# Order of the seven block products of a channel pair in the SwiGLU up-projection: t1 third, and in the first pair h22 ahead of t3

## Chip, cores and metric

One core of one Trainium2 chip. The metric is the device time of one execution in microseconds (us); the kernel before was run three times.

## The reference, cut to what matters

One decoder layer: a Mamba-2 and a sparse-attention mixer, an output projection, a layer norm, and a SwiGLU channel mixer with a causal convolution of width 3, for 1024 tokens, width 1024 and 2816 gate and 2816 up channels, in float32.

```python
def _conv_ffn(h, w_up, conv_w, conv_b, w_down):
    u = _causal_dwconv(h @ w_up, conv_w, conv_b)
    gate, up = jnp.split(u, 2, axis=-1)
    return (jax.nn.silu(gate) * up) @ w_down
```

The change lies in how `h @ w_up` is computed.

## The kernel before, in words

**The product.** `h @ w_up` is done by a scheme of the Strassen-Winograd kind with seven block products in place of eight. The blocks of h are h11 and h21 (tokens 0 to 511, the two halves of the 1024 inputs), h22 (the second half of the inputs for tokens 512 to 1023) and the differences t1 (block 4 to 7 less block 0 to 3, first half of the inputs), t2, t3 and t4. The blocks of the weights are, for each of 22 channel pairs j (128 gate columns g and 128 up columns u), the halves of g and u and the sums of them that `w_prep` forms on VectorE: s13 = (u0 + u1, g0 - u0), s24 = (s13's first - g0, g1 - s24's first), in lines 1051 to 1054.

**Precision.** Every operand is split into a high part (a rounded copy, on ScalarE) and a low part (the difference, on VectorE or GpSimd). A product is four input blocks of 128, each with three matmuls of 128x128 by 128x512 (`three`, lines 159 to 161), so 12 matmuls, and 84 a pair. `w_split` (lines 956 to 962) splits one weight block: ScalarE line 960, GpSimd line 961.

**Banks.** A pair uses a bank `pa` for h11 and h21 (`first`), `pb` for t2, `pc` for t3 and t4, and `pd` for t1 and h22. The first product in `pc` or `pd` is read by VectorE, and then the second is accumulated onto it in the same bank. These readings (evictions) are issued by `now` (line 978), with a priority 300 places ahead of their place in the program. Their results u2 and u3 lie in 128x512 buffers of the tag "s2", of which there are five; c1 (line 984), hr, d1, d3 and d4 use the same tag.

**Before the pairs.** The second part of the layer norm makes h for eight token blocks (lines 991 to 1043) and writes the operands h11, h21, t1, t2, h22 with `put`: line 922 on ScalarE, line 923 on VectorE or GpSimd. `first` of pairs 0 and 1 is already issued there, and `w_prep(0)` follows. Lines 1066 to 1072 then make t3 (d3, line 1069, VectorE) and t4 (d4, line 1071, GpSimd) from t2's raw values and h_raw.

**Weights and buffers.** `up_load` (line 938) loads the raw g and u of a pair, 512 KB each, on SP's queue, into three buffers of the tag "wr". `w_split` number n takes its buffer by a list (the lines quoted first below), three buffers of "wh", three of "wl" and eight of "pp", of which t1 holds four, and h_raw four until the d4 that reads it is done. Numbers 0 to 3 are the halves of g of pairs 0 and 1, so pair 0's other five blocks are numbers 4 to 8 in the order of the loop in `w_prep`, with the tags wh, wl, wh, wl, pp.

```python
WTAG = ("tx", "tx", "wh", "wl", "wh", "wl", "wh", "wl", "pp", "pp", "wh", "wl", "pp", "pp")
t = big("w_hl", F32R, (P, 2, 512), WTAG[n] if n < 4 else WTAG[4 + (n - 4) % 10])
```

**Order.** A planner fixes each engine's instruction order ahead of the run: it walks through its own timeline of the program and gives a free engine the instruction of highest priority (earliest in the program) that is ready in that timeline. SP's queue alone keeps the order of the program. On the chip each engine works through its queue in the fixed order.

**After the products** of a pair, `conv_half` (lines 1074 to 1084) takes a bias and three taps (ScalarE line 1078, VectorE line 1082 twice) of `xu` and `xg`, for each half of 512 tokens, then SiLU (line 1115) and the product with the up half (line 1116). Every second pair also forms sums of the gated values on VectorE and GpSimd (lines 1125 to 1136) and stores them for the down-projection.

Of the kernel before, what the change touches and what calls it, by code (L numbers as in the profile page):

```python
# [13 lines left out]
OP = mybir.AluOpType  # L14
# [43 lines left out]
def hybrid_layer(ctx, tc, x, w_in, ssd_conv_w, ssd_conv_b, dt_bias, a_log, d_skip, ssd_norm_g,  # L58
                 idx_k_norm_g, idx_k_norm_b, w_out, ln1_g, ln1_b, w_up, ffn_conv_w, ffn_conv_b,
                 w_down, ln2_g, ln2_b, out):  # L60
    nc = tc.nc
# [15 lines left out]
    def big(name, dtype=F32, shape=(P, 1024), tag="t4"):  # L77
        return pool.tile(list(shape), dtype, name=name, tag=tag, bufs=BUFS[tag])

    def bank(name, tag, shape=(P, 512)):  # L80
        return psum.tile(list(shape), F32, name=name, tag=tag, bufs=PBUFS[tag])
# [4 lines left out]
    def mid(name, dtype=F32, shape=(P, 512), tag="s2"):  # L86
        return pool.tile(list(shape), dtype, name=name, tag=tag, bufs=S2 if tag == "s2" else EV)

    def f(t):
        return t.bitcast(F32)  # L90
# [67 lines left out]
    def three(ps, ah, al, bh, bl, start, stop, onto=False):  # L158
        nc.tensor.matmul(ps, ah, bh, start=start, stop=False, skip_group_check=onto)  # L159
        nc.tensor.matmul(ps, ah, bl, start=False, stop=False, skip_group_check=onto)  # L160
        nc.tensor.matmul(ps, al, bh, start=False, stop=stop, skip_group_check=onto)  # L161
# [269 lines left out]
    def next_w(ahead=1):  # L431
        load_ahead(1)
        w = ready.pop(0)
        load_ahead(ahead)
        return w
# [3 lines left out]
    for t in range(4):  # L439
        w = w_qi if t == 0 else next_w()  # L440
        a, c = big("qsa", F32R, tag="pp"), big("qsb", F32R, tag="pp")
# [472 lines left out]
    def operand(name, tag):  # L914

        return [[big(name + p, F32R, (P, 2, 512), tag) for _ in range(2)] for p in "hl"]
# [17 lines left out]
    def pair_of(n):  # L934

        return n // 2 + n % 2 * (NF // 2)

    def up_load(j, parts=(0, 1)):
        if j < NF:
            raws.setdefault(j, [])  # L940
            ct = pair_of(j)
            for s in parts:
                raw = big("w_raw", tag="wr", shape=(P, NK, P))
                nc.sync.dma_start(raw, bass.AP(tensor=w_up.tensor, offset=w_up.offset + s * DFF + ct * P,
                                               ap=[[2 * DFF, P], [P * 2 * DFF, NK], [1, P]]))
                raws[j].append(raw)

    def up_gate(j):

        g = raws[j][0].rearrange("p (k2 k) n -> p k2 (k n)", k2=2)  # L950
        return [w_split(g[:, k2]) for k2 in range(2)]
# [4 lines left out]
    def w_split(src):  # L956
        n = count["w"]
        count["w"] += 1
        t = big("w_hl", F32R, (P, 2, 512), WTAG[n] if n < 4 else WTAG[4 + (n - 4) % 10])
        nc.scalar.activation(t[:, 0], src, AF.Copy)  # L960
        nc.gpsimd.tensor_tensor(t[:, 1], src, f(t[:, 0]), op=OP.subtract)  # L961
        return t
# [8 lines left out]
    def product(ps, w, h, start):  # L971

        for k in range(4):
            ks = slice(k * P, (k + 1) * P)
            three(ps, w[:, 0, ks], w[:, 1, ks], h[0][k // 2][:, k % 2], h[1][k // 2][:, k % 2],
                  start and k == 0, k == 3, not start)

    def now(call, *a, **k):
        with tc.high_priority(EV_PRIO):
            call(*a, **k)  # L980

    def first(j, w):

        a, c1 = bank("pa", "ip"), mid("c1")
        product(a, w[0], h11, True)
        now(nc.scalar.activation, c1, a, AF.Copy)
        product(a, w[1], h21, False)
        return a, c1

    firsts = {}  # L990
    for i, b in enumerate(LN_ORDER):
# [7 lines left out]
        if i == 4:  # L999
            t2_raw += [big("t2raw", tag="tx") for _ in range(2)]  # L1000
            h22, t1, t2 = operand("h22", "t4"), operand("t1", "pp"), operand("t2", "t4")
            up_load(0)
        if i == 5:
            gates = {0: up_gate(0)}
# [42 lines left out]
    def w_prep(j):  # L1047

        g, u = (t.rearrange("p (k2 k) n -> p k2 (k n)", k2=2) for t in raws.pop(j))
        s13, s24 = big("s13", tag="pt", shape=(P, 2, 512)), big("s24", tag="pt", shape=(P, 2, 512))  # L1050
        nc.vector.tensor_tensor(s13[:, 0], u[:, 0], u[:, 1], op=OP.add)
        nc.vector.tensor_tensor(s24[:, 0], s13[:, 0], g[:, 0], op=OP.subtract)
        nc.vector.tensor_tensor(s13[:, 1], g[:, 0], u[:, 0], op=OP.subtract)
        nc.vector.tensor_tensor(s24[:, 1], g[:, 1], s24[:, 0], op=OP.subtract)
        if j not in gates:
            gates[j] = [None, None]
        out = []
        for src, w in ((g[:, 0], gates[j][0]), (s24[:, 0], None), (g[:, 1], gates[j][1]), (s13[:, 1], None),
                       (s13[:, 0], None), (u[:, 1], None), (s24[:, 1], None)):
            out.append(w or w_split(src))  # L1060
        return out

    ws = {0: w_prep(0)}
    up_load(1, (1,))
    t3, t4 = operand("t3", "wo"), operand("t4", "wo")
# [8 lines left out]
    def conv_half(x_, tag, ct, half):  # L1074

        v_ = bank("v", tag)
        o = half * 512
        nc.scalar.activation(v_, x_[:, o:o + 512], AF.Identity, bias=fw[:, 132 + ct:133 + ct], scale=fw[:, 88 + ct:89 + ct])
        for sft in (1, 2):
            tap = fw[:, (2 - sft) * 44 + ct:(2 - sft) * 44 + ct + 1]  # L1080
            z = 0 if half else sft
            nc.vector.scalar_tensor_tensor(v_[:, z:], x_[:, o - sft + z:o + 512 - sft], tap, v_[:, z:],
                                           op0=OP.mult, op1=OP.add)
        return v_

    for j in range(NF):
        if j:
            up_load(j + 1)
        w = ws.pop(j)
        a, c1 = firsts.pop(j) if j in firsts else first(j, (w[0], w[2]))  # L1090
        bb = bank("pb", "pv")
        product(bb, w[1], t2, True)
        xg, xu, gt = big("xg", tag="tx"), big("xu", tag="tx"), big("gt", tag="t4")
        u2 = mid("u2")
        now(nc.vector.tensor_tensor, u2, c1, bb, op=OP.add)
        now(nc.scalar.activation, xg[:, :512], a, AF.Copy)
        c = bank("pc", "tp")
        product(c, w[3], t3, True)
        u3 = mid("u3")
        now(nc.vector.tensor_tensor, u3, u2, c, op=OP.add)  # L1100
        d = bank("pd", "lg")
        product(d, w[4], t1, True)
        now(nc.vector.tensor_tensor, xu[:, 512:], u3, d, op=OP.add)
        product(c, w[5], t4, False)
        now(nc.vector.tensor_tensor, xu[:, :512], u2, c, op=OP.add)
        product(d, w[6], h22, False)
        now(nc.vector.tensor_tensor, xg[:, 512:], u2, d, op=OP.add)
        if j + 1 < NF:
            ws[j + 1] = w_prep(j + 1)
        cg, cu = pair_of(j), NF + pair_of(j)  # L1110
        for half in range(2):
            hs = slice(half * 512, half * 512 + 512)
            vu = conv_half(xu, "lg", cu, half)
            vg = conv_half(xg, ("ip", "tp")[half], cg, half)
            nc.scalar.activation(gt[:, hs], vg, AF.Silu)
            nc.vector.tensor_tensor(gt[:, hs], gt[:, hs], vu, op=OP.mult)
        rows = slice(j // 2 * P, (j // 2 + 1) * P)
        if j % 2 == 0:
            v1 = gt
            nc.scalar.dma_start(g_dr[rows, 0], v1[:, :512])  # L1120
        else:
            lo1, hi1, lo2, hi2 = v1[:, :512], v1[:, 512:], gt[:, :512], gt[:, 512:]
            nc.scalar.dma_start(g_dr[rows, 1], lo2)
            q1, q2 = mid("q1", tag="ev"), mid("q2", tag="ev")
            nc.vector.tensor_tensor(q1, hi1, hi2, op=OP.add)
            nc.vector.tensor_tensor(q2, q1, lo1, op=OP.subtract)
            q3, q4 = hi1, lo1
            nc.gpsimd.tensor_tensor(q3, lo1, hi1, op=OP.subtract)
            nc.gpsimd.tensor_tensor(q4, lo2, q2, op=OP.subtract)
            nc.scalar.dma_start(g_dr[rows, 2], q4)  # L1130
            for n, (q, hi) in enumerate(((q1, xu[:, :512]), (q2, xu[:, 512:]), (q3, xg[:, :512]), (hi2, xg[:, 512:]))):
                hi, lo = hi.bitcast(F32R), q.bitcast(F32R)
                nc.scalar.activation(hi, q, AF.Copy)
                nc.gpsimd.tensor_tensor(lo, q, f(hi), op=OP.subtract)
                nc.scalar.dma_start(gs_dr[rows, 0, n], f(hi))
                nc.scalar.dma_start(gs_dr[rows, 1, n], f(lo))
# [107 lines left out]
    c1, u2 = ([x[t // 2][:, t % 2] for t in range(4)] for x in (cu, uu))  # L1244
    u3 = c1
# [79 lines left out]
```

## Time and profile before

| what | value |
|---|---|
| three runs, us | 1696.53, 1702.73, 1699.14; median 1699.14 |
| the profiled execution, us | 1697.82 |
| its span, first to last instruction, us | 1695.9 |
| mean granted TensorE clock over the span | 0.974 of 2.4 GHz |
| TensorE matmul busy | 1595.1 us, 94% |
| VectorE busy | 1250.8 us, 74% |
| ScalarE busy | 926.1 us, 55% |
| GpSimd busy | 896.0 us, 53% |

The products of the 22 pairs run from about 1009 us to 1466 us of the span; the down-projection follows to the end. In the rows, times are from the start of the span. Engines: PE is TensorE, PEld its weight load, DVE VectorE, ACT ScalarE, POOL GpSimd, SPq SP's DMA queue. "out<-in" names the tiles; a bracket at the end of a row gives the engine's idle time before it and what ended that. Names are shortened in the records: `s` is s13 or s24, `d` is d1, d3 or d4 (the line tells which), `u` is u2 or u3.

### The profile page before, as it was taken

What the parts mean: (1) busy time and instruction counts of PE and PEld (TensorE: products, weight loads), DVE (VectorE), ACT (ScalarE), POOL (GpSimd) and SP (SyncE); (2) the same over time, 40 slices, a digit from 0 to 9 for tenths busy, and PEclk for the clock granted to TensorE, in tenths of its full rate; (3) what the DMA queues carried; (4) which work ended last, traced back from release to release, by engine and by line L of the source; (5) the groups of instructions that cost most, each with busy time, mean ns of one, the idle gap of its engine ahead of it and who ended that gap; (6) DMA issues with size and microseconds to landing.
All of it is one profiled execution on the core that took longest, in us unless ns stands there. A gap on an engine that the chain in (4) does not pass through costs nothing.

```text
span 1695.9 us, 23283 instructions
## 1 busy us (share of the span) xinstructions
PE 1595.1 (94%) x7844; PEld 1318.0 (78%) x7844; DVE 1250.8 (74%) x2262; ACT 926.1 (55%) x1809; POOL 896.0 (53%) x669
## 2 busy tenths in 40 slices
PE   8999998897989989999999995999999999989997
PEld 6888887685878867777888774888888788868886
DVE  2644689999894457787787579668777777678668
ACT  3433597687732576676676465555455555542141
POOL 2153225534168253555464448586776667576590
PEclk9999999997999999999999997999999999999999
DMA  5042032132423563554454461243433333698782
GB/s 173 10 129 63 13 106 85 41 99 57 140 83 108 176 200 108 148 156 133 137 156 156 140 193 55 94 137 130 147 122 118 118 128 117 220 371 304 234 283 106
DMA packets 208590, 232.86 MB, mean 137 GB/s; under 512 B 14035, under 2 KB 138327, under 8 KB 208471
## 3 DMA queue, kind: packets, MB, share of 16 engines
q1 hardware_dynamic: 161031, 159.80, 31.3%
q10 hardware_dynamic: 47440, 71.58, 11.5%
q8 instruction: 62, 1.02, 0.3%
q14 instruction: 57, 0.47, 0.1%
HBM read 159.71 MB, written 71.63 MB: 136 GB/s over the span
## 4 chain that ended last, share of the span: by engine, by line
PE 67%; DVE 20%; DMA 4%; ACT 4%; issue 3%; POOL 2%; ACTq 0%; SPq 0%; DVEq 0%; POOLq 0%
PE proj L159 4%; PE proj L161 4%; PE proj L160 4%; PE acc L160 4%; PE acc L161 4%; PE acc L159 4%; DVE junk L347 3%; PE ops L159 3%; PE ops L160 3%; PE ops L161 3%; PE ptp L692 3%; PE pc L160 2%; PE pc L161 2%; PE pc L159 2%; PE pd L159 2%
## 5 line engine op out<-in xcount | busy, mean ns | idle before, releaser
L159 PE MATMUL proj<-xTh,w_hi 128*128 128x512 f32 (+1 forms) x432 | 173.1, 401 | 7.2 <-ACT xbc L478 4.6
L161 PE MATMUL proj<-xTh,w_lo 128*128 128x512 f32 (+1 forms) x432 | 170.5, 396 | 3.0 <-POOL w_lo L132 3.0
L686 POOL TENSOR_SCALAR prob<-prob,sm 128x512 f32<-128x512 f32 (+7 forms) x128 | 96.5, 763 | 143.9 <-DVE sm L685 109.2
L160 PE MATMUL proj<-xTl,w_hi 128*128 128x512 f32 (+1 forms) x432 | 171.2, 397 | 0.0
L961 POOL TENSOR_TENSOR w_hl<-s,w_hl 128x512 fp32r<-128x512 f32 x88 | 119.4, 1364 | 72.1 <-ACT w_hl L960 68.9
L129 POOL TENSOR_SCALAR w_hi<-w_raw 128x1024 fp32r<-128x1024 f32 x35 | 44.3, 1267 | 184.3 <-PE proj L160 125.5
L132 POOL TENSOR_TENSOR w_lo<-w_raw,w_hi 128x1024 fp32r<-128x1024 f32 (+1 forms) x45 | 112.5, 2503 | 27.7 <-ACT w_hi L131 25.5
L160 PE MATMUL acc<-wd_hl,g_hl 128*128 128x512 f32 x308 | 121.6, 395 | 3.6 <-POOL wd_hl L1205 3.6
L161 PE MATMUL acc<-wd_hl,g_hl 128*128 128x512 f32 x308 | 121.2, 394 | 0.0
L683 ACT ACTIVATE prob<-prob,mx 128x512 f32<-128x512 f32 (+7 forms) x128 | 98.4, 770 | 36.5 <-DVE mx L680 35.8
L694 ACT ACTIVATE pt<-ptp 128x512 fp32r<-128x512 f32 x144 | 81.2, 594 | 64.8 <-PE ptp L692 43.5
L159 PE MATMUL acc<-wd_hl,g_hl 128*128 128x512 f32 x308 | 112.6, 393 | 2.8 <-ACT wd_hl L1204 2.7
L961 POOL TENSOR_TENSOR w_hl<-w_raw,w_hl 128x512 fp32r<-128x512 f32 x66 | 91.2, 1386 | 41.7 <-ACT w_hl L960 40.8
L1205 POOL TENSOR_TENSOR wd_hl<-keep,wd_hl 128x512 fp32r<-128x512 f32 x55 | 92.0, 1704 | 33.9 <-ACT wd_hl L1204 33.9
L159 PE MATMUL ops<-w_hi,y_hi 128*128 128x512 f32 x256 | 104.2, 407 | 5.6 <-ACT y_hi L131 3.1
L350 ACT ACTIVATE junk<-score,cand 128x1024 bf16<-128x1024 f32 (+2 forms) x96 | 86.0, 896 | 39.7 <-DVE cand L364 36.7
L695 DVE TENSOR_TENSOR pt<-ptp,pt 128x512 fp32r<-128x512 f32 x144 | 95.5, 684 | 15.1 <-ACT pt L694 14.8
L159 PE MATMUL tps<-w_hi,xTh 128*128 128x256 f32 x320 | 96.0, 301 | 9.8 <-ACT tout L614 8.7
L160 PE MATMUL ops<-w_lo,y_hi 128*128 128x512 f32 x256 | 102.8, 402 | 0.4 <-DVE w_lo L132 0.4
L159 PEld LDWEIGHTS proj<-xTh,w_hi 128*128 128x128 f32 (+1 forms) x432 | 82.0, 190 | 27.0 <-ACT xbc L478 5.4
L161 PE MATMUL ops<-w_hi,y_lo 128*128 128x512 f32 x256 | 100.4, 396 | 0.0
L161 PEld LDWEIGHTS proj<-xTh,w_lo 128*128 128x128 f32 (+1 forms) x432 | 81.6, 189 | 21.2 <-POOL w_lo L132 4.2
(344 smaller groups left out, 5057.8 us busy)
## 6 DMA issues: line engine op xcount, KB each, us to landing
w_raw<-in_ffn_w_up_dram SPq DMA_DIRECT2D x44, 512.0 KB, 3.9
g_hl<-gs_dr SPq DMA_DIRECT2D x44, 512.0 KB, 5.0
w_raw<-in_w_in_dram SPq DMA_DIRECT2D x36, 512.0 KB, 4.4
r_dr<-rout ACTq DMA_DIRECT2D x48, 256.0 KB, 2.3
g_dr<-gt ACTq DMA_DIRECT2D x33, 256.0 KB, 2.9
keep<-in_ffn_w_down_dram SPq DMA_DIRECT2D x33, 256.0 KB, 6.1
acsb<-a_dr SPq DMA_DIRECT2D x16, 512.0 KB, 4.1
w_raw<-in_w_out_dram SPq DMA_DIRECT2D x16, 512.0 KB, 3.8
```

The costliest lines, as they stand in the source:

```text
L132: (nc.vector if lo_on_dve else nc.gpsimd).tensor_tensor(lo, raw, f(hi), op=OP.subtract)
L159: nc.tensor.matmul(ps, ah, bh, start=start, stop=False, skip_group_check=onto)
L160: nc.tensor.matmul(ps, ah, bl, start=False, stop=False, skip_group_check=onto)
L161: nc.tensor.matmul(ps, al, bh, start=False, stop=stop, skip_group_check=onto)
L347: nc.vector.tensor_scalar(junk[0][:, :n], top[b] if k >= 16 and b in top else score_ap[b], c, None, op0=OP.is_lt, op1=OP.add, accum_out=va ...
L350: nc.scalar.activation(junk[1][:, :n], score_ap[b], AF.Sign, bias=c, scale=-1.0, accum_out=val[e][:, i:i + 1])
L683: nc.scalar.activation(t[:, :w], t[:, :w], AF.Exp, bias=mx[:, h:h + 1], scale=-1.0, accum_out=sm[:, h:h + 1])
L686: nc.gpsimd.tensor_scalar(t[:, :w], t[:, :w], sm[:, 4 + h:5 + h], 1.0, op0=OP.mult, op1=OP.mult)
L694: nc.scalar.activation(pt[:, 0], ps, AF.Copy)
L695: nc.vector.tensor_tensor(pt[:, 1], ps, f(pt[:, 0]), op=OP.subtract)
L961: nc.gpsimd.tensor_tensor(t[:, 1], src, f(t[:, 0]), op=OP.subtract)
L1205: nc.gpsimd.tensor_tensor(wt[:, 1], w_raw, f(wt[:, 0]), op=OP.subtract)
```

## The change

The loop in `w_prep` splits the weight blocks in another order, and the pair loop issues the products in another order. Before: t2, t3, t1, t4, h22 (behind h11 and h21). After: t2, t1, t3, h22, t4; in pair 0: t2, t1, h22, t3, t4. u3 is now u2 plus the t1 product, where it was u2 plus the t3 product. The last product of a pair is t4, whose eviction writes `xu[:, :512]`; before it was h22, whose eviction writes `xg[:, 512:]`. The instructions are as many as before.

```diff
-        for src, w in ((g[:, 0], gates[j][0]), (s24[:, 0], None), (g[:, 1], gates[j][1]), (s13[:, 1], None),
-                       (s13[:, 0], None), (u[:, 1], None), (s24[:, 1], None)):
+        for src, w in ((g[:, 0], gates[j][0]), (s24[:, 0], None), (g[:, 1], gates[j][1]), (s13[:, 0], None),
+                       (s24[:, 1], None), (s13[:, 1], None), (u[:, 1], None)):
             out.append(w or w_split(src))
         return out
...
         now(nc.scalar.activation, xg[:, :512], a, AF.Copy)
+        d = bank("pd", "lg")
+        product(d, w[3], t1, True)
+        u3 = mid("u3")
+        now(nc.vector.tensor_tensor, u3, u2, d, op=OP.add)
         c = bank("pc", "tp")
-        product(c, w[3], t3, True)
-        u3 = mid("u3")
-        now(nc.vector.tensor_tensor, u3, u2, c, op=OP.add)
-        d = bank("pd", "lg")
-        product(d, w[4], t1, True)
-        now(nc.vector.tensor_tensor, xu[:, 512:], u3, d, op=OP.add)
-        product(c, w[5], t4, False)
+        if j:
+            product(c, w[5], t3, True)
+            now(nc.vector.tensor_tensor, xu[:, 512:], u3, c, op=OP.add)
+        product(d, w[4], h22, False)
+        now(nc.vector.tensor_tensor, xg[:, 512:], u2, d, op=OP.add)
+        if not j:
+            product(c, w[5], t3, True)
+            now(nc.vector.tensor_tensor, xu[:, 512:], u3, c, op=OP.add)
+        product(c, w[6], t4, False)
         now(nc.vector.tensor_tensor, xu[:, :512], u2, c, op=OP.add)
-        product(d, w[6], h22, False)
-        now(nc.vector.tensor_tensor, xg[:, 512:], u2, d, op=OP.add)
```

## Rows read from the trace of the kernel before

**Rows 1.** Windows: length, busy us (x instructions) by engine, clock, DMA share, GB/s

```profile
1041.00:1062.14 21.14, 10.91 (x27) 7.06 (x26) 18.57 (x18) 8.04 (x22) 20.08 (x16) 0.68 0.09 26
...
1062.14:1338.00 275.86, 275.84 (x1215) 227.47 (x1213) 207.65 (x285) 150.39 (x247) 191.70 (x144) 1.00 0.38 128
```

**Rows 2.** Waits of PE, 1030 to 1470 us: total us, times, longest

```profile
PE pc L159 <- ACT t3h L922: 6.5, 1, 6.5
...
PE pb L160 <- DVE t2l L923: 2.9, 1, 2.9
PE pd L159 <- DVE xg L980: 1.6, 1, 1.6
PE pb L161 <- POOL w_hl L961: 1.1, 1, 1.1
```

**Rows 3.** Timeline of PE: start us, us, engine, line, operation

```profile
1057.07 0.79 PE L159 MATMUL pc<-t3h,w_hl 128*128 128x512 f32 x1 [6.51 <-ACT t3h L922]
...
1062.14 0.39 PE L159 MATMUL pb<-t2h,w_hl 128*128 128x512 f32 x1
...
1064.86 0.39 PE L159 MATMUL pd<-h22h,w_hl 128*128 128x512 f32 x1
...
1070.52 0.39 PE L159 MATMUL pb<-t2h,w_hl 128*128 128x512 f32 x1
```

**Rows 4.** Chain of waits: start us, its share of the chain in us, what

```profile
1039.80 0.75 DVE s L1051
...
1041.15 0.60 DVE s L1053
...
1048.66 1.14 DVE s L1052
...
1051.49 1.13 DVE s L1054
1052.62 2.28 DVE t3l L923 x2
...
1056.60 0.42 ACT t3h L922
```

**Rows 5.** Timeline of POOL

```profile
1017.08 1.71 POOL L961 TENSOR_TENSOR w_hl<-w_raw,w_hl 128x512 fp32r<-128x512 f32 x1
...
1042.85 0.90 POOL L923 TENSOR_TENSOR h22l<-hr,h22h 128x256 fp32r<-128x256 f32 x1
1043.71 1.44 POOL L961 TENSOR_TENSOR w_hl<-s,w_hl 128x512 fp32r<-128x512 f32 x1
```

**Rows 6.** Timeline of DVE

```profile
1047.92 0.75 DVE L923 TENSOR_TENSOR t3l<-d,t3h 128x256 fp32r<-128x256 f32 x2
...
1059.50 0.69 DVE L980 TENSOR_TENSOR u<-c,pb 128x512 f32<-128x512 f32 x1
...
1469.33 0.74 DVE L1082 SCALAR_TENSOR_TENSOR v<-xu,fw,v 128x512 f32<-128x512 f32 x1
```

**Rows 7.** Timeline of ACT

```profile
1041.30 0.41 ACT L922 ACTIVATE t3h<-d 128x256 fp32r<-128x256 f32 x1
...
1042.92 0.63 ACT L960 ACTIVATE w_hl<-s 128x512 fp32r<-128x512 f32 x1 [0.60 <-POOL d L1071]
```

**Rows 8.** Timeline of SP's queue: issues of raw up-projection weights

```profile
1018.81 0.38 SPq L944 DMA_DIRECT2D w_raw<-in_ffn_w_up_dram  x1
1024.15 0.38 SPq L944 DMA_DIRECT2D w_raw<-in_ffn_w_up_dram  x1
1033.38 0.37 SPq L944 DMA_DIRECT2D w_raw<-in_ffn_w_up_dram  x1
```

**Rows 9.** Tile w_raw, 1000 to 1470 us: from issue to landing

```profile
DMA to landing us min/median/max: 3.8/3.9/4.6
```

**Rows 10.** Timeline of PE at the start of the down-projection

```profile
1487.55 0.51 PE L160 MATMUL acc<-wd_hl,g_hl 128*128 128x512 f32 x1 [3.61 <-POOL wd_hl L1205]
```

**Rows 11.** Waits of all engines, 1075 to 1440 us: total us, times, longest

```profile
DVE s L1051 <- DMA w_raw<-in_ffn_w_up_dram: 24.4, 17, 3.5
```

## The prediction

> **What bounds the kernel now.** I read the windows over the up-projection stage first. From 1062 us to 1338 us TensorE issues 1215 matmuls in 275.86 us, one every 0.227 us, with no idle time [rows 1]. A pair is 84 matmuls, or 19.1 us, and the change removes none, so in that stretch there is only work that cannot be shortened by reordering. What an order can win or lose is idle time, and the waits of TensorE list it [rows 2]: 6.5 us ahead of the first t3 product, 1.6 and 1.1 us at about 1340 us, and smaller waits for t1 and t2. The reader should see that the only large hole is ahead of pair 0's t3. Next I read the order of TensorE's queue. The wait of 6.51 us ends at 1057.07 us; the twelve t3 matmuls end at 1062.14, and pair 0's h22 starts only at 1064.86, behind pair 1's t2 [rows 3]. Last I followed the chain of waits back from t3. It runs on VectorE from 1039 to 1057 us, ends in the last t3 high part on ScalarE and the last t3 low part on VectorE [rows 4], and it contains four instructions that t3 does not need: the weight sums of pair 2 (L1051, L1053, L1052, L1054), 0.75 + 0.60 + 1.14 + 1.13 = 3.62 us. They stand there because that pair's raw weights were already loaded.
>
> **The change, part by part.** No instruction is added or removed: seven products, the same evictions, and seven splits per pair as before. The sum therefore has only terms of order.
>
> h22 ahead of t3 in pair 0. Its operand is complete when the last h22 low part ends on GpSimd at 1043.75 [rows 5], 13 us before t3. But it accumulates onto the bank of t1, so it has to wait until t1 has been read by the new u3 = u2 + d, and u2 comes first. On VectorE u2 of pair 0 runs at 1059.50, straight behind the last t3 low part [rows 6]. I explain the place by the five buffers of the tag "s2": two hold c1 of pairs 0 and 1, three hold the differences d3 and d4, and u2 starts as the last d3 is used up. The change leaves those buffers alone. Then h22 cannot start before u2 and u3 are written, about 1061 us, and t3 is ready earlier. Taken at 0; the hole is not filled by h22 (the other end is a rival below). From 1062 us the queue is full either way, so moving h22 ahead of t2 of pair 1 gains nothing there.
>
> The order of the splits. This is the part I expect to act. Split number n takes its buffer by a fixed list of tags, and the fifth split of pair 0 has tag "pp", where all eight buffers are held by t1 (four) and by h_raw (four). Before, the fifth is s24's second half, and it waits for the first d4 to free h_raw: 1042.92 on ScalarE, released by L1071 [rows 7]. u's second half was the fourth and was split on GpSimd at 1017.08 to 1018.79; the load issued at 1018.81 takes the raw buffer that it freed [rows 5, 8]. After the change u's second half is the fifth. It is split at about 1043.7 to 1045.2, where s24 is now [rows 5], and pair 0's raw u stays occupied until then. The loads that follow move down the free buffers: u of pair 1 from 1018.81 to 1024.15 (g's buffer of pair 0), g of pair 2 from 1024.15 to 1033.38, u of pair 2 from 1033.38 to about 1045.2 [rows 8]. A load lands 3.9 us after its issue [rows 9], so u of pair 2 is there at 1049.1 and not at 1037.3, and L1051 of pair 2 cannot run at 1039.80.
>
> What follows for t3. The weight sums of pair 2 stand after t3's work in the program, so where they are not ready in time the planner takes t3's instructions first. The four leave the chain, but not all of the 3.62 us comes back. The second t3 low part of block 4 needs its high part, which ScalarE ends at 1041.71 [rows 7]: of L1051 and L1053 (1.35 us) I take 1.2. L1052 comes back whole, 1.14. Behind L1054 stands the same kind of wait, 0.42 us for a high part [rows 4], so 0.7 of 1.13. Sum 1.2 + 1.14 + 0.7 = 3.0 us, with 0 and 3.62 as its ends: t3 starts at about 1054 us, and TensorE is 3.0 us ahead from there. I take a value near the upper end because VectorE's chain is without gaps in [rows 4]. What hides the four once they are late: t2 of pair 2, their first user, started at 1070.52 [rows 3], and needs one sum, one split and one low part after them, under 5 us.
>
> These instructions have no fixed time: the two t3 low parts at 1047.92 took 0.75 us together, the two at 1052.62 took 2.28 us [rows 4, 6]. The Trainium skill, SBUF — State Buffer, section Who interferes with whom, says that a VectorE instruction with two SBUF inputs and a GpSimd instruction that reads SBUF exclude each other, the later one waiting for the whole of the earlier. By that rule the waits would pass to t3's own instructions and the four would be worth only their undisturbed time, about 0.7 us each or 2.7 us in all, as an estimate. The trace agrees with the rule as far as the spread from 0.75 to 2.28 us goes; which GpSimd instruction was met is not shown there.
>
> The clock. The twelve t3 matmuls take 5.07 us [rows 3] where twelve at 0.227 us are 2.72: 2.3 us go to the half clock after the hole. The hole shrinks from 6.5 to 3.5 us. The nearest row is the wait of 2.9 us ahead of the t2 matmul at 1045.49, after which the half clock also shows in the mean of 0.68 for 1041 to 1062 us [rows 1, 2]. So I take no gain, and keep 2.3 us as an end.
>
> All later pairs: t1, t3, h22, t4 for t3, t1, t4, h22. TensorE stays full as long as evictions come in time. The 1.61 us wait at 1343 us is t1 waiting for the eviction of the pair before's h22 [rows 2]. h22 is now one product (2.72 us) further from the next t1, which would cover it; but u's first half is now evicted last, and both halves of u's convolution stand behind it. I set these against each other: 0, with -2.7 (both waits gone) and +2.7 for each new stall of that kind.
>
> The end of the stage. The last pair's gate is finished up to 1.5 us later (two more taps on VectorE at 0.74 us [rows 6] behind the last eviction), and GpSimd's work on it stands ahead of a weight split for which TensorE already waits 3.61 us [rows 10]. VectorE has other work to interleave there, so I take 0 and keep 1.5.
>
> Sum: -3.0 us. The profiled execution took 1697.82 us, of which the span is 1695.9; the sum gives 1694.8. The median of the three runs stands 1.32 us above that execution, so against the median 1699.14 - 3.0 = 1696.1 us.
>
> **The rivals.** (a) Slower: VectorE waits for the load. The planner lets VectorE stand at L1051 for a raw load in 17 pairs, 24.4 us in all [rows 11]. If L1051 of pair 2 keeps its place ahead of t3's low parts, it waits from 1039.8 to 1049.1: 9.3 us later for t3, 1708.4 us. It decides from the place of L1051 in VectorE's queue: behind the third d3 (L1069) it costs nothing. Against it: t3 comes first in the program, and the landing moves by 12 us, more than the planner is likely to overlook. (b) h22 fills the hole: u2 and u3 get buffers earlier, and twelve matmuls move ahead of t3. That saves 12 x 0.227 = 2.7 us: 1696.4. For it speaks the operand's time, against it u2's place on VectorE. (c) The change does nothing: other work takes the four places, or the u load finds a buffer in time: 1699.1. (d) The later pairs get worse: the gate of each odd pair comes later, GpSimd's queue stands longer, raw loads and evictions follow, as at 1338 us, where 2.7 us were lost [rows 2]. Three such stalls less the gain of 3.0 are +5.1: 1704.2.
>
> **How the numbers follow.** Chances: the forecast 0.42, (a) 0.15, (b) 0.12, (c) 0.20, (d) 0.11. A measurement of this kernel tells 0.3%, about 5.1 us, from no change, so faster means below 1694.0 and slower above 1704.2. Faster needs the forecast or (b) together with the two waits at 1340 us gone or the clock regained: about two in five of 0.54, and a little of (c): 0.25. Slower is most of (a) and half of (d): 0.19. The rest, 0.56, is the same. The range: below, 3.6 + 2.3 + 2.7 = 8.6 us of gains, 1690.5; above, it goes past (d), which leaves out most of (a): 1705.5.
>
> **What would show it.** Right: the load of pair 2's u is issued at about 1045 us in the new time, L1051 of pair 2 stands behind the third or fourth d3 on VectorE, and the wait ahead of pair 0's t3 is about 3.5 us. u2 and u3 of pair 0 run back to back behind the last t3 low part. Wrong: h22 matmuls between t2 and t3; an idle VectorE at L1051 waiting for a raw load before t3; the third wait of 6.5 us unchanged; or new TensorE waits between 1062 and 1466 us, where there are now only two.

## The result, and the profile after

The kernel after takes 1708.47 us (median of five runs, 1704.53 to 1708.95), the kernel before 1699.14 (1696.53 to 1702.73, five runs on the same chip). The ratio is 1.0052, 95% interval 1.0041 to 1.0063: about 9 us slower. The forecast was 1696.1, and 1708.5 lies above its range, which ended at 1705.5.

The profiled execution has a span of 1705.8 us, 9.9 more than before. Where these 9.9 us are is read from three views. First the start of the pairs on TensorE, to set beside [rows 3]:

```profile
1051.28 0.80 PE L159 MATMUL pc<-t3h,w_hl 128*128 128x512 f32 x1 [4.47 <-ACT t3h L922]
...
1053.38 0.79 PE L160 MATMUL pc<-t3l,w_hl 128*128 128x512 f32 x1 [1.30 <-DVE t3l L923]
...
1057.69 0.40 PE L159 MATMUL pb<-t2h,w_hl 128*128 128x512 f32 x1
...
1060.45 0.39 PE L159 MATMUL pd<-h22h,w_hl 128*128 128x512 f32 x1
```

Pair 0's t3 is done and t2 of pair 1 starts at 1057.69, where it was 1062.14: **4.45 us gained**. h22 of pair 0 still stands behind t3 and behind t2 of pair 1. From t2 of pair 1 to the first matmul of the down-projection, TensorE has the same 1766 matmuls in both kernels. The windows over that stretch, before and after (length, then busy us and instructions of PE, PEld, DVE, ACT, POOL; clock, DMA share, GB/s), the kernel before first:

```profile
1062.14:1466.20 404.06, 401.33 (x1766) 330.58 (x1764) 303.98 (x418) 216.14 (x355) 274.08 (x203) 1.00 0.40 131
```

```profile
1057.69:1477.18 419.49, 404.85 (x1766) 331.30 (x1764) 309.63 (x419) 216.54 (x359) 275.18 (x208) 1.00 0.38 128
```

The stretch is **15.43 us longer**: idle time grows from 2.73 to 14.64 us (+11.9), and the same matmuls are busy 3.5 us longer, about half of it behind one wait (last section). The down-projection then starts 11.0 us later (-4.45 + 15.43). What follows it took 229.7 us and takes 228.6. The sum, +9.9, is the growth of the span. The waits of TensorE in the kernel after, 1062 to 1478 us (total us, times, longest), name what it idles for; in [rows 2] this stretch had only the 1.6 and the 1.1 us:

```profile
PE pd L159 <- DVE u L980: 9.8, 7, 2.7
PE pc L159 <- DVE xu L980: 3.2, 1, 3.2
PE pa L159 <- ACT c L980: 1.7, 2, 1.2
```

The first line is h22, to be accumulated onto t1's bank, waiting for u3 to read that bank. One of the seven, in pair 9, in TensorE's timeline (the last t1 matmul and the first h22) and in VectorE's (u3):

```profile
1230.71 0.39 PE L161 MATMUL pd<-t1h,w_hl 128*128 128x512 f32 x1
...
1238.76 0.50 PE L159 MATMUL pd<-h22h,w_hl 128*128 128x512 f32 x1 [2.67 <-DVE u L980]
```

```profile
1238.03 0.68 DVE L980 TENSOR_TENSOR u<-u,pd 128x512 f32<-128x512 f32 x1
```

u3 starts 6.9 us after the end of t1's last matmul. Between the two products TensorE has only the rest of t3 and h11, about 5 us. The kernel before has the same kind of place: u3 reads t3's bank, and t4 is accumulated onto it. Its pair 9, again TensorE first:

```profile
1227.92 0.39 PE L161 MATMUL pc<-t3h,w_hl 128*128 128x512 f32 x1
...
1233.81 0.39 PE L159 MATMUL pc<-t4h,w_hl 128*128 128x512 f32 x1
```

```profile
1232.67 0.67 DVE L980 TENSOR_TENSOR u<-u,pc 128x512 f32<-128x512 f32 x1
```

u3 is written at 1233.34 and t4 starts at 1233.81, without a wait, 0.47 us later. From the same three rows of the other pairs, this margin was 0.4 to 0.7 us in seven of the eight odd pairs 5 to 19. A list of waits doesn't show it. After the change u3 starts 5.0 to 6.9 us behind the end of t1 in pairs 7, 8, 9, 17 and 19, and h22 waits in each of them. In pairs 3 and 21, the other two of the seven waits (1.5 and 0.8 us), u3 is not as late (2.4 us and 0.04), but h22 comes sooner behind t1 on TensorE. A small margin is not the whole account: pairs 5, 11 and 13 had 0.4 to 0.6 us before and don't wait after, while pairs 3, 8 and 21 had 1.3 to 3.9 us and do.

What makes u3 late is read from the chain of waits of the kernel after that ends in this h22, from 1222.86 us on (start, share of the chain in us, what):

```profile
1222.86 1.30 POOL gt L1133
1224.16 1.25 POOL gt L1138
1225.41 1.26 POOL w_hl L961
...
1226.68 3.73 DMA w_raw<-in_ffn_w_up_dram
...
1230.70 1.44 issue
...
1232.28 1.57 issue
1233.85 0.67 DVE gt L1120
...
1235.77 1.68 DVE s L1052
1237.45 0.67 DVE v L1082
1238.11 0.60 DVE u L980
1238.71 0.04 issue
1238.76 0.50 PE pd L159
```

GpSimd forms an odd pair's sums and their low parts (L1133 and L1138, which were L1129 and L1134 before the change), then the low part of a split; that frees a raw buffer, and the load takes 3.73 us. The two longer "issue" pieces (1.44 and 1.57 us) are VectorE at the weight sums L1051 and L1053 that needed the load (1230.51 and 1232.14, 1.7 us each); gate products, taps and L1052 stand before u3 in its queue. Five more of its waits for u3 end chains of this form. It looks like rival (d), so the experiments begin with the places and then take this chain apart.

### The profile page after: what moved, and what is told of

Its sections match the earlier page's. It is cut to its first block, busy times and chain, and to the rows that moved or that the text cites. A ratio compares the mean times of both kernels' runs of the same rounds, so it can differ in the third digit from the quotient of the medians.

```text
span 1705.8 us, 23274 instructions
## 1 busy us (share of the span) xinstructions
PE 1596.6 (94%) x7844; PEld 1319.2 (77%) x7844; DVE 1243.2 (73%) x2262; ACT 925.4 (54%) x1809; POOL 886.6 (52%) x669
## 4 chain that ended last, share of the span: by engine, by line
PE 57%; DVE 23%; issue 5%; DMA 5%; POOL 5%; ACT 4%; SPq 0%; DVEq 0%; ACTq 0%; POOLq 0%
DVE junk L347 4%; PE proj L159 4%; PE proj L161 4%; PE proj L160 4%; PE acc L159 3%; PE acc L160 3%; PE acc L161 3%; PE ops L159 3%; PE ops L161 3%; PE ops L160 3%; PE ptp L692 3%; DMA w_raw<-in_ffn_w_up_dram 2%; DVE conv L484 2%; POOL w_hl L961 2%; PE pv L698 2%
```

## The experiments

The ratios are to the kernel before on the same chip, with 95% intervals. "Waits in the stage" are TensorE's, summed over its list from 1062 us to the first matmul of the down-projection: 2.7 us before, 14.7 after.

**Which half of the change.** Four kernels: the new split order with the old products (the products take their blocks by new numbers); the new products with the old splits; both in pair 0 alone; and all of it without pair 0's exception.

```diff
-        product(c, w[3], t3, True)
+        product(c, w[5], t3, True)
...
-        product(d, w[4], t1, True)
+        product(d, w[3], t1, True)
```

That is splits_only against the kernel before, whose loop in `w_prep` is the one of the kernel after (t4 and h22 take w[6] and w[4] likewise). products_only has the pair loop of the kernel after, with t1, t3, h22, t4 on w[4], w[3], w[6], w[5]. first_pair_only chooses both by j, and no_exception takes the two branches of pair 0's exception out of the kernel after (the first is shown, `if not j` goes too):

```diff
+        first = ((s13[:, 0], None), (s24[:, 1], None), (s13[:, 1], None), (u[:, 1], None))
+        later = ((s13[:, 1], None), (s13[:, 0], None), (u[:, 1], None), (s24[:, 1], None))
+        for src, w in ((g[:, 0], gates[j][0]), (s24[:, 0], None), (g[:, 1], gates[j][1])) + (later if j else first):
```

```diff
-        if j:
-            product(c, w[5], t3, True)
-            now(nc.vector.tensor_tensor, xu[:, 512:], u3, c, op=OP.add)
+        product(c, w[5], t3, True)
+        now(nc.vector.tensor_tensor, xu[:, 512:], u3, c, op=OP.add)
```

> New order of the splits in all pairs, products in the old order. Theory (product order costs): the early t3 of pair 0 without the waits of h22, 1693 to 1698 us. Rival (the late split of u frees the raw buffers late, so that VectorE stands at the weight sums with u3 behind them): 1703 to 1710 us, with TensorE waiting for u3 in several pairs.

> New order of the products in all pairs, splits in the old order. Theory (product order costs): the wait of about 6.5 us ahead of pair 0's t3 is back and the waits of h22 for u3 stay, 1707 to 1714 us. Rival (late split of u): 1697 to 1702 us.

> New splits and new products in pair 0 alone, pairs 1 to 21 as before. Theory: the gain sits in pair 0 (its t3 starts 5.8 us sooner, 4.4 us of it kept at t3's end) and the loss in the product order of the later pairs, so 1693 to 1697 us, with a wait of 3 to 5 us ahead of pair 0's t3 and no waits of h22 for u3. Rival (the h22 exception of pair 0 is what costs): 1703 us or more. Rival (scatter of the planner): anything from 1696 to 1708, with waits in other places than before.

> The changed kernel, but pair 0 in the order of the other pairs (t3 ahead of h22). Theory: h22 of pair 0 stood behind t3 in TensorE's queue anyway, so the start is the same and the time within 2 us of the changed kernel's, 1706 to 1711. Rival (the exception of pair 0 costs): 1695 to 1702 us.

| kernel | median us | ratio | waits in the stage |
|---|---|---|---|
| splits_only | 1697.75 | 0.9997 (0.9987 to 1.0006) | 5.1 |
| products_only | 1699.04 | 1.0001 (0.9991 to 1.0012) | 4.6 |
| first_pair_only | 1702.12 | 1.0021 (1.0007 to 1.0034) | 5.6 |
| no_exception | 1708.34 | 1.0057 (1.0041 to 1.0073) | 14.4 |

By the whole time either half alone costs nothing and the two together cost 9 us: an interaction. The theory that the product order alone costs (1707 to 1714 for products_only) fails, and so does its rival, the late split alone (1703 to 1710 for splits_only). The exception of pair 0 has no part in it: in no_exception TensorE's matmuls come in the same order as in the kernel after, all 7844 of them. In splits_only t3 starts at 1051.38, as after the change, and in products_only at 1057.46, as before: the gain at the start belongs to the split order.

In the stage the halves are not free, though. From t2 of pair 1 to the down-projection the profiled executions take 408.2 us in splits_only and 407.7 in products_only, 4.2 and 3.7 us more than the 404.06 before, against 15.4 more with both halves. splits_only had gained as much at its start (t2 of pair 1 at 1057.93).

first_pair_only missed its 1693 to 1697. Its t3 starts at 1050.90, but then TensorE waits 2.97 us more for the last t3 low part, since VectorE has L1052 ahead of it there, and t2 of pair 1 starts at 1059.53, 2.6 us sooner than before. The stretch behind it is 407.8 us, 3.7 longer than before, though pairs 1 to 21 are in the old orders: its waits are mostly of the two kinds that the kernel before has, 3.2 us for `xg` and 2.0 for a split. Why they grew was not traced.

**The wait itself.** In no_bank_read u3 is formed without reading t1's bank, so h22 has nothing to wait for; the control does the same to the kernel before.

```diff
-        now(nc.vector.tensor_tensor, u3, u2, d, op=OP.add)
+        now(nc.vector.tensor_tensor, u3, u2, u2, op=OP.add)
```

> The changed kernel with u3 = u2 + u2 in place of u2 plus the t1 bank: VectorE does as many instructions, but h22 no longer has to wait until t1's bank has been read (t1's share is missing from one block of the output). Theory (TensorE's waits of h22 for u3, 9.8 us in the profile, are most of the loss): those waits vanish and the time falls by 7 to 12 us, to 1696 to 1702. Rival (VectorE is late as a whole, and the next reader of a bank, xu or xg, holds TensorE instead): 1704 to 1709 us with waits for xu or xg.

> Control for the run without the bank's reading: the kernel before with u3 = u2 + u2, so that t4 need not wait until t3's bank has been read (t3's share is missing from one block of the output). Theory (the waits for u3 are what the changed kernel loses, and the kernel before has next to none): 1692 to 1699 us, at most 5 us less than the kernel before. Rival (the edit itself is worth some 18 us by lighter work or another plan): 1685 or less.

no_bank_read: 1690.24 us, 0.9960 (0.9947 to 0.9973). The control: 1695.76, 0.9984 (0.9974 to 0.9995). The waits of TensorE in no_bank_read, same stretch, are gone but for 0.7 us, those for `xu` and `c` too:

```profile
PE pd L159 <- DVE gt L1120: 0.4, 1, 0.4
PE pa L159 <- ACT w_hl L960: 0.3, 1, 0.3
```

The edit is worth 0.92% (1.0052 less 0.9960, some 16 us) to the kernel after and 0.16% (3 us) to the kernel before. Without that reading, the change makes the kernel faster: 0.9960 / 0.9984 = 0.9976, or 4.1 us, about the 4.45 us gained at the start. So **the reading of t1's bank by u3 carries the loss**. The time fell further than the 1696 to 1702 that was expected. The edit takes away two things at once, h22's wait for u3 and u3's own wait for t1, and the planner writes another order for it. u3's own wait is the smaller candidate: VectorE waits for t1 there for only 1.3 us in all in the kernel after, against the 9.8 us of TensorE.

**Which place in the split order.** With the new products, the splits in two further orders: t1, t3, t4, h22 (u's second half third of these four, as before the change), and t3, t1, h22, t4 (u's last, as after). In `mixed` only pair 0 has the new splits, by `first` and `later` as above; first_splits_only has these and the old products. The loop of swap_t1_t3, and then that of t4_last, against the kernel after (the products' numbers follow):

```diff
-                       (s24[:, 1], None), (s13[:, 1], None), (u[:, 1], None)):
+                       (s13[:, 1], None), (u[:, 1], None), (s24[:, 1], None)):
```

```diff
-        for src, w in ((g[:, 0], gates[j][0]), (s24[:, 0], None), (g[:, 1], gates[j][1]), (s13[:, 0], None),
-                       (s24[:, 1], None), (s13[:, 1], None), (u[:, 1], None)):
+        for src, w in ((g[:, 0], gates[j][0]), (s24[:, 0], None), (g[:, 1], gates[j][1]), (s13[:, 1], None),
+                       (s13[:, 0], None), (s24[:, 1], None), (u[:, 1], None)):
```

> New products in all pairs; splits t1, t3, t4, h22, that is t1's and t3's exchanged and u's second half where it was. Theory (u's second half as the last split is what makes the new products slow, since it frees the raw buffer late): as the run with the products alone, 1697 to 1702 us, t3 of pair 0 waits 6 us or more again. Rival (the exchange of t1's and t3's splits costs): 1704 to 1710.

> New products in all pairs; splits t3, t1, h22, t4, that is u's second half last and t3 ahead of t1 as before. Theory (u's second half last costs): 1704 to 1710 us, with pair 0's t3 early and waits of h22 for u3 of about 10 us. Rival: 1693 to 1699, the early t3 without the waits.

> New products in all pairs, new splits in pair 0 alone (later pairs split u's second half third, as before). Theory (the early t3 comes from pair 0's splits, the loss from u's second half split last in the later pairs): the early t3 of pair 0 without the long waits of h22 for u3, 1693 to 1698 us. Rival (an earlier start runs into the same late u3): 1702 or more.

> Old products in all pairs, new splits in pair 0 alone. Theory: t3 of pair 0 about 5 us sooner and the later pairs as before, 1692 to 1697 us. Rival (what is won at the start is lost again at the raw loads, as the run with all splits new came out at 1697.75): 1697 to 1700.

| kernel | u's second half | median us | ratio | waits in the stage |
|---|---|---|---|---|
| swap_t1_t3 | third | 1697.35 | 1.0000 (0.9989 to 1.0010) | 5.1 |
| mixed | third, last in pair 0 | 1696.62 | 0.9991 (0.9983 to 1.0000) | 4.1 |
| first_splits_only | third, last in pair 0 | 1699.86 | 1.0013 (1.0004 to 1.0022) | 5.7 |
| t4_last | last | 1722.59 | 1.0151 (1.0130 to 1.0172) | 20.1 |

With the new products, the two kernels with u's half last in all pairs lose (14.7 and 20.1 us of waits) and the others don't. The plainest pair is mixed and the kernel after: the same products, the same splits in pair 0, and the split order of pairs 1 to 21 alone makes 1696.62 us (0.9991) or 1708.47 (1.0052). Two forecasts failed: t4_last lies 13 us above its 1704 to 1710, and first_splits_only above its 1692 to 1697, where its rival was. In first_splits_only t3 starts at 1053.34, but behind a wait of 3.0 us for the last t3 low part t2 of pair 1 starts only 1.0 us sooner than before (1061.13), and the stretch behind it is 4.0 us longer. What is waited for is not always u3. In t4_last it is first of all ScalarE's copy of bank `pa` (waits of TensorE, 1062 to 1487 us):

```profile
PE pa L159 <- ACT xg L980: 10.0, 2, 5.0
PE pd L159 <- DVE u L980: 5.7, 3, 2.2
PE pa L159 <- ACT c L980: 4.4, 5, 1.4
```

**The chain, link by link.** Four kernels, each the kernel after with one edit: evictions with less priority; one weight sum on GpSimd instead of VectorE; the low part of u's last split on VectorE instead of GpSimd; the first and third weight sums from g alone, so that they don't need the u load (with a control). Their first changed lines, in this order; in the last kernel the third sum becomes `g[:, 0]` less `g[:, 1]` likewise:

```diff
-EV_PRIO = 300
+EV_PRIO = 200
...
-        nc.vector.tensor_tensor(s13[:, 1], g[:, 0], u[:, 0], op=OP.subtract)
+        nc.gpsimd.tensor_tensor(s13[:, 1], g[:, 0], u[:, 0], op=OP.subtract)
...
-            out.append(w or w_split(src))
+            out.append(w or w_split(src, nc.vector if len(out) == 6 and j else None))
...
-        nc.vector.tensor_tensor(s13[:, 0], u[:, 0], u[:, 1], op=OP.add)
+        nc.vector.tensor_tensor(s13[:, 0], g[:, 0], g[:, 1], op=OP.add)
```

> The changed kernel with evictions 200 places ahead in place of 300, which makes the planner order other instructions anew and changes nothing else. Theory (the loss belongs to the order itself): 1704 to 1711 us with h22 waiting for u3 in at least five pairs. Rival (scatter of the planner): 1695 to 1703, or waits in wholly other places.

> The changed kernel with one of the four weight sums (L1053) on GpSimd in place of VectorE. Theory (u3 is late because VectorE works off weight sums and taps ahead of it): u3 is due sooner, the waits of h22 for u3 fall below 6 us, 1698 to 1704 us. Rival (GpSimd's own queue sets the raw loads and splits): 1706 us or more.

> The kernel after, with the low part of the last split (u's second half, pairs 1 to 21) on VectorE instead of GpSimd: 21 instructions of about 0.7 to 1.7 us change engines, the raw buffer of u no longer waits for GpSimd's queue. Theory (GpSimd's queue releases the raw buffer late): the waits of SP's loads for a split fall from 273 us to below 220, u3's waits from 9.8 to below 5 us, time 1697 to 1704. Rival (VectorE's own load decides; it gets up to 35 us more work): u3's waits grow past 10 us and the time past 1710.

> The kernel after, with the first and third weight sums formed from the two halves of g instead of from g and u (so the products are of other weights; instructions as many and of the same shapes). VectorE's sums then need only the g load, which is issued ahead of the u load. Theory (the late raw u load holds VectorE's queue, and u3 stands behind it): the waits of VectorE at L1051 for a raw load shrink below 5 us in all, u3's lag falls under 5.2 us in nearly all pairs, the waits of TensorE for u3 fall from 9.8 us to below 3, and the time is 1695 to 1700. Rival (u3 is late by the number of sums, taps and splits between it and the product's end, whatever the load does): waits for u3 stay at 7 us or more and the time at 1705 to 1710.

> Control: the kernel before with the same two sums formed from g alone. Both theories: within 4 us of the kernel before, 1694 to 1701, since the waits for the raw load (24.4 us of VectorE) cost TensorE nothing there. If it gains as much as sums_from_g gains on the kernel after, the edit itself is worth that and says nothing of the change.

| kernel | median us | ratio | waits in the stage | of these for u3 |
|---|---|---|---|---|
| ev200 | 1708.22 | 1.0070 (1.0053 to 1.0087) | 14.4 | 9.7 |
| sums_on_pool | 1710.20 | 1.0071 (1.0055 to 1.0087) | 14.5 | 9.0 |
| u_low_on_dve | 1706.55 | 1.0049 (1.0035 to 1.0064) | 12.9 | 4.2 |
| sums_from_g | 1702.37 | 1.0015 (1.0005 to 1.0025) | 13.1 | 2.6 |
| sums_from_g_before | 1693.98 | 0.9977 (0.9968 to 0.9987) | 2.3 | 0.7 |

ev200 tests nothing: all four engines run the same instructions in the same order as in the kernel after, so it is a repeat, and it repeats the time (1708.22 and 1708.47). sums_on_pool missed its theory, waits for u3 below 6 us; its rival's 1706 or more came. No single link, as far as these edits cut it, is the cause. u_low_on_dve and sums_from_g did bring u3's waits down, as their theory had it, and the time didn't follow: the waits went to the next eviction. These are the waits of TensorE in u_low_on_dve, 1062 to 1479 us:

```profile
PE pc L159 <- DVE xu L980: 6.1, 2, 3.3
PE pd L159 <- DVE u L980: 4.2, 4, 1.7
PE pa L159 <- ACT c L980: 2.6, 2, 1.7
```

And in sums_from_g, which is still 0.38% slower than its control (1.0015 / 0.9977 = 1.0038):

```profile
PE pc L159 <- DVE xu L980: 6.2, 5, 2.5
PE pa L159 <- ACT c L980: 4.3, 1, 4.3
PE pd L159 <- DVE u L980: 2.6, 3, 1.3
```

sums_from_g didn't even take the load's wait away: VectorE stands at L1051 for a raw load for 40.7 us in all (19.5 in the kernel after), where the theory had under 5. As a test of the load it is inconclusive. Nor did u_low_on_dve free the raw buffers sooner: SP's queue waits 125.7 us for GpSimd's splits and 156.5 for VectorE's, 282 where it was 273 and below 220 was expected.

**The raw buffer or the split's own buffer.** u_from_sum lets the last split of pairs 1 to 21 read the first weight sum, which frees the raw u buffer earlier (with a control). tags_shift keeps every operation and every operand of the kernel after, and only moves the list of buffer tags on for the splits behind pair 0's. Their edits against the kernel after:

```diff
-                       (s24[:, 1], None), (s13[:, 1], None), (u[:, 1], None)):
+                       (s24[:, 1], None), (s13[:, 1], None), (s13[:, 0] if j else u[:, 1], None)):
...
-        t = big("w_hl", F32R, (P, 2, 512), WTAG[n] if n < 4 else WTAG[4 + (n - 4) % 10])
+        t = big("w_hl", F32R, (P, 2, 512), WTAG[n] if n < 4 else WTAG[4 + (n - 4 + (7 if n > 8 else 0)) % 10])
```

> The kernel after, where the last split of pairs 1 to 21 reads the first weight sum in place of u's second half (products of other weights; instructions as many and of the same shapes). The raw u buffer is then free after L1053, well ahead of the last split. Theory (the raw u buffer held by the last split delays the next load and with it the sums and evictions): SP's waits for a split fall from 273 us to under 200, the waits of TensorE in the stage from 14.7 to under 6 us, time 1694 to 1699. Rival (the load does not matter; the splits' buffers or the plan do): TensorE's waits stay above 10 us, time 1703 to 1710.

> Control: the kernel before with the same edit of the split of u (there the sixth of seven). Both theories: within 4 us of the kernel before, 1695 to 1702, TensorE's waits in the stage under 6 us.

> The kernel after, with the list of buffer tags moved on by seven places for pairs 1 to 21, so that each split takes the tag of another place in the list; nothing else. Theory (the raw load): TensorE's waits in the stage stay at 12 to 17 us, time 1705 to 1711. Rival (which buffers the splits take decides): the waits fall below 8 us or rise above 20, and the time moves by more than 5 us from 1708.

u_from_sum: 1693.89 us, 0.9972 (0.9963 to 0.9982), waits in the stage 5.9 us, SP's waits for a split 105.7 us. That was expected by the theory of the raw load, but the control gained too, 1689.92 us, 0.9952 (0.9940 to 0.9965), outside its 1695 to 1702; against it 0.20% of the 0.52% is left. tags_shift: **1694.46 us, 0.9980 (0.9971 to 0.9989)**, 0.72% (12 us) below the kernel after and, if by little, faster than the kernel before: the fastest of the kernels that compute the layer as it is. Its list of TensorE's waits (1000 to 1500 us) has one line for that stretch, and ahead of it the hole at the start, which is larger here:

```profile
PE pc L159 <- ACT t3h L922: 8.6, 1, 8.6
PE pd L159 <- DVE u L980: 4.4, 6, 1.3
```

That bears on the raw loads. SP's queue, 1075 to 1430 us, waits for the splits to free raw buffers as long in tags_shift as after the change; the two rows, the kernel after first:

```profile
SPq L944 <- POOL w_hl L961: 273.5, 35, 17.5
```

```profile
SPq L944 <- POOL w_hl L961: 274.0, 33, 17.6
```

This sum tells how long the queue stood, not how late the loads came: in splits_only it is 270.8 us as well. How late they came is told by the time from the issue of a pair's raw u to the pair's first t2 matmul, here the mean of pairs 3 to 21: 22.4 us in the kernel before, 19.1 after, 18.8 in tags_shift, 26.1 in splits_only. In tags_shift the loads come as late as after the change, and 10 of the 12 us of new waits are gone. It is the rival's outcome: other buffers for the splits, with the order that the planner writes for them.

**What is shown and what stays open.** Shown: the loss is TensorE waiting for evictions; it needs the new product order, in which h22 stands behind u3 on t1's bank, and the new split order in pairs 1 to 21; late raw loads do not suffice; with the tags moved nearly all of it is gone. Open is by which split and which buffer the evictions become late, whether it is u's half last or s24's no longer last, and whether other tags would help the kernel before as much: moving the tags makes the planner write another order for every engine, so tags_shift doesn't part the buffer from the order that goes with it.

## Why the prediction was wrong, point by point

**The start: the way was right, the size larger than forecast.** The load of pair 2's raw u is issued at 1043.39 (forecast 1045.2, before 1033.38 [rows 8]), as u's second half is now split at 1041.96 to 1043.36. L1051 of pair 2 stands behind the third d3. VectorE's timeline after the change:

```profile
1047.11 0.69 DVE L1069 TENSOR_TENSOR d<-t2raw,hraw 128x512 f32<-128x512 f32 x1
...
1048.96 0.69 DVE L1051 TENSOR_TENSOR s<-w_raw 128x512 f32<-128x512 f32 x1
1049.57 1.21 DVE L1069 TENSOR_TENSOR d<-t2raw,hraw 128x512 f32<-128x512 f32 x1
1050.70 1.75 DVE L1053 TENSOR_TENSOR s<-w_raw 128x512 f32<-128x512 f32 x1
1052.38 2.36 DVE L923 TENSOR_TENSOR t3l<-d,t3h 128x256 fp32r<-128x256 f32 x2
1054.85 0.69 DVE L980 TENSOR_TENSOR u<-c,pb 128x512 f32<-128x512 f32 x1
1055.57 0.69 DVE L980 TENSOR_TENSOR u<-u,pd 128x512 f32<-128x512 f32 x1
```

L1052 and L1054 have left the way to t3, L1051 and L1053 have not, yet the gain is 4.45 us against 3.0 and an upper end of 3.62. The third and the fourth d3 and the last t3 low parts before the change:

```profile
1049.73 1.76 DVE L1069 TENSOR_TENSOR d<-t2raw,hraw 128x512 f32<-128x512 f32 x1
...
1054.93 1.63 DVE L1069 TENSOR_TENSOR d<-t2raw,hraw 128x512 f32<-128x512 f32 x1
1057.04 2.35 DVE L923 TENSOR_TENSOR t3l<-d,t3h 128x256 fp32r<-128x256 f32 x2 [0.48 <-ACT t3h L922]
```

The last t3 low part ends at 1054.74, before at 1059.39: 4.65 us. Of these, 0.96 are there at the first d3 already (it starts at 1036.26, before at 1037.22), 2.27 are the two sums that left [rows 4], and 1.4 lie in what stayed: the third and fourth d3 take 0.69 and 1.21 us, before 1.76 and 1.63, while L1053 takes 1.75, before 0.68. The first and the last of these parts were in no term of the sum, so that the gain passed its upper end was luck. t3 itself starts at 1051.28 (forecast about 1054), behind a wait of 4.47 us (forecast about 3.5) and with 1.30 more behind its first matmul.

u2 and u3 run back to back behind the last t3 low part, as said, so h22 has no place in the hole: that step and the refusal of rival (b) hold. That the five buffers of "s2" are the reason, no run tests.

**"All later pairs": the step that failed.** It stood at 0, with 2.7 us for each new stall. It was worked out from the waits that the kernel before had, two of them, and weighed only the new product order, by the distance from an eviction to the next pair. The new split order had a term for pair 0 alone and none for pairs 1 to 21; mixed, which keeps the old splits there, takes 1696.62 us, so the loss needs just what the sum left out. Nor did it ask how much room the evictions had that were in time: u3's 0.4 to 0.7 us in most odd pairs. The product that follows u3 onto its bank was changed from t4 to h22 and the bank from t3's to t1's, and u3 was put behind other work. Measured: +15.43 us between t2 of pair 1 and the down-projection, 11.9 of it idle and 3.5 in matmuls at a lower pace.

**The clock.** The hole shrank and no gain was counted, which fits: over pair 0's t3 the granted clock is 0.55 after the change (1051.28 to 1057.69 us) and was 0.59 (1057.07 to 1062.14). But the clock has a term of its own in the longest of the new stalls, which the prediction had priced at its idle time alone (see the last section).

**The end of the stage.** Taken as 0, with 1.5 as an end: what follows the first matmul of the down-projection took 1.1 us less. TensorE's waits for weight splits there are 6.3 us in both kernels: the longest before are 3.61 at [rows 10] and 2.24, after it is 4.79, for ScalarE's half of a split. As forecast, within the bounds.

**The rivals.** (a) was excluded by the place of L1051; its 1708.4 us agrees with the result for no reason of its own. (c) fell with the start. (d) is the nearest: it named the odd pairs' GpSimd work, raw loads and evictions, and the chain above runs that way. It counted three stalls of 2.7 us; there were ten waits, 14.7 us. And its mechanism is not the whole: with loads that come as late, tags_shift stalls for 4.4 us in all. The chances of 0.11 for it and 0.19 for slower rested on a bound for the later pairs that came from waits already there. The text did name new waits of TensorE between 1062 and 1466 us as what would prove it wrong.

## What to carry to other kernels

Before reordering work that feeds an engine without idle time, list the margins as well as the waits: for every buffer or bank that is reused, the time from its reader's end to its next writer's start. Margins of half a microsecond, in a stage of 22 repetitions, are places where a new order can stall, and they appear in no list of waits; they don't tell which will, as four of the seven waits for u3 came in pairs with such a margin. Give every part of the change a term in every stage it touches: here the new split order had one in pair 0 alone. Test the halves of a reordering apart and together, since here each was neutral in time alone, and read the stage beside the whole, where neither was free. And if the loss moves to another eviction with every edit, try another assignment of buffers before giving the order up: here that edit gave 12 us back.

## What the runs showed of the hardware

One stall cost more than its idle time. In the kernel after the wait of 3.21 us for `xu` ends at 1346.19 us, and the windows over the matmuls that follow show the clock. The third row is the same view behind the 2.67 us wait of pair 9:

```profile
1346.19:1349.50 3.31, 3.31 (x10) 2.59 (x11) 3.12 (x5) 3.31 (x6) 1.79 (x2) 0.65 0.20 79
1349.50:1353.00 3.50, 3.50 (x15) 2.83 (x14) 3.50 (x6) 0.99 (x2) 1.86 (x2) 0.85 0.20 75
1238.76:1242.00 3.24, 3.24 (x14) 2.69 (x15) 1.94 (x4) 1.74 (x5) 2.55 (x2) 1.00 0.39 114
```

The granted clock is 0.65 and then 0.85 of 2.4 GHz, between its two levels of 1.2 and 2.4 GHz: the windows hold matmuls that start 0.43 us apart (1347.28 to 1349.84 us) beside others 0.23 apart. The twelve t3 matmuls behind the wait run from 1346.19 to 1350.64, 4.45 us where twelve at 0.227 [rows 1] are 2.72, so this wait cost 1.7 us on top of its 3.21. Behind the wait of 2.67 us the clock stayed at 1.00.

VectorE's weight sums are as uneven as [rows 4, 6] had them: L1051 takes 0.69 us at 1048.96 and L1053, of the same shape, 1.75 us at 1050.70. The Trainium skill, SBUF — State Buffer, section Who interferes with whom, says that a VectorE instruction with two SBUF inputs, as these are, and a GpSimd instruction reading SBUF wait for each other. The spread from 0.69 to 1.75 us agrees with it; no run here isolated the two.
